# A hybrid attention block on one core: transfers issued in program order, value products in three parts, one product moved from VectorE to GpSimd

## The chip, the cores and the metric

The kernel runs on one core of a Trainium2 chip. The metric is the device time of one execution in microseconds. Three executions of the kernel before took 2690.57, 2697.05 and 2703.49 us; their median is 2697.05 us.

## What is computed

One layer of a transformer-like block over 2048 tokens of width 1024, all in float32. Cut to what matters here:

```python
def stick_breaking_attention(q, k, v):          # 4 heads, causal, head width 64
    # A[t,s] = sigmoid(z_ts) * prod_{s<j<t} (1 - sigmoid(z_tj)),  z = q.k / sqrt(d)
    ...
def chunked_relpos_attention(q, k, v, rel_bias): # 8 heads, chunks of 64, a band of 576 keys
    probs = jax.nn.softmax(scores, axis=-1)
    out = jnp.einsum('bhcqk,bhckd->bhcqd', probs, vb)
    ...
proj = rmsnorm(x, attn_norm_w) @ w_in
y = group_rmsnorm(concat([y_sb, y_ch, y_cv]), out_norm_w)   # y_cv: a gated depthwise convolution
x = x + y @ w_out
x = x + swiglu(rmsnorm(x, ffn_norm_w), w_gate, w_up, w_down)
```

Products keep nearly float32 accuracy by splitting each operand into a high and a low float16 part and adding three of the four partial products.

## The kernel before

**Two halves.** The host hands the tokens over in reversed order, and the kernel works through them in two halves of 1024 (`HALVES`, L50), each of two groups of 512. Everything up to the first half's output projection runs in one interleaved stage, `weave` (L941): two streams of work are traced piece by piece, and TensorE executes exactly that order, since `tc.manual_schedule(engines={PE})` (L1015) fixes it. VectorE, ScalarE, GpSimd and the SyncE queue that issues all transfers are not fixed: a scheduler in the framework puts their instructions in the order that its own model of time suggests, and may take a load long ahead of the place where the program names it. After `weave` come the first half's feed-forward part, the second half's output projection and its feed-forward part (L1102 to L1106), where nothing is fixed by hand.

**The first stream, `fill` (L900),** holds the projections: for each half V, Q and K of the heads, the convolution, then the first half's output projection. Weights are loaded, scaled and split into two float16 parts by `Weights.split` (L227); the parts go to DRAM (L277) to be read again for the second half (L236). Activations are loaded four tiles at a time by `Rows.ahead` (L435; `x_rows`, `y_rows`, `ffn_rows` say from where), normalised where a gain belongs to them (`rms_rows`, L364) and transposed on TensorE (`to_T`, L321). Q and K parts are stored by `put_parts` (L526), V parts by `v_block` (L535). A small clock counts this stream's TensorE work; `later(after, what)` (L895) traces a step so many of its microseconds further on.

**The second stream, `attend` (L788),** holds the attention: per half 12 heads (4 stick-breaking, then 8 chunked), per head two groups, per group four tiles of 128 queries. It loads K, V and, for chunked heads, a bias at the head's start (L798 to L806), and two arrangements of the queries in four transfers at each group's start (L818). A tile of a stick-breaking head is cut into pieces of up to four key blocks; a chunked tile is one piece. In `weave`, `stage` gives each piece three beats; in each beat every open piece that is due goes one step on, and a third of the piece's share of `fill` is traced. A piece's first products are traced at the start of the third beat of its stage, so two beats after the loads that `attend` named just before it.

**A stick-breaking piece (`stick_tile`, L713):** scores on TensorE, two sigmoids on ScalarE (L730, L731), a running product over the remainders by a scan on VectorE (L733), then the product of sigmoids and shifted remainders, `MUL` (L735, `nc.vector` by L53). The remainder tile `re` starts with a memset on GpSimd (L727). Five beats later the product is transposed on TensorE (L660) and split into a high part by ScalarE (L664) and a low part by VectorE (L669), in `turned`.

**The product with the values (`weighted`, L673)** comes five beats after that. For each key block the high part multiplies V's two parts side by side (128 columns, L679) and the low part multiplies V's high part (64 columns, L684). `put_y` (L689) copies and scales the sum one beat later on ScalarE (L694), and another beat later GpSimd adds its two halves of 64 columns (L696) and the tile's result is stored (L697). Two `yu` buffers and one PSUM bank `av` serve this. A chunked tile's scale `f` (L776) has four buffers.

**The output projection (`out_proj`, L858)** loads the residual `xs` where it reads the accumulator (L868, two buffers) and stores the sum at once (L872).

Of the kernel before, what the change touches and what calls it, by code (L numbers as in the profile page):

```python
# [9 lines left out]
F32 = mybir.dt.float32  # L10
# [5 lines left out]
ALU = mybir.AluOpType  # L16
# [24 lines left out]
def trunk(ctx: ExitStack, tc: tile.TileContext, x, anw, w_in, qnw, knw, biasx, conv_w, onw, w_out,  # L41
# [10 lines left out]

    MUL = nc.vector  # L53
    SH_T = ("k c", dict(k=KT))
# [61 lines left out]
    def acc():  # L116
        return bank("acc", 2)
# [86 lines left out]
    class Weights:  # L204
# [22 lines left out]
        def split(self, n):  # L227
# [43 lines left out]
            for i, raw in enumerate(tiles):  # L271
                yield 1.5
                w = wp.tile([128, 2, D], F16, name="w16", tag="w16")
                nc.scalar.activation(raw, raw, AF.Copy, scale=sc[:, 0:1] if one else sc[:, i:i + 1])  # L274
                nc.scalar.copy(w[:, 0, :], raw)  # L275
                nc.gpsimd.tensor_tensor(w[:, 1, :], raw, w[:, 0, :], ALU.subtract)  # L276
                nc.sync.dma_start(wd[key][i], w)  # L277
                made.append(w)
# [204 lines left out]
    def y_rows(H, groups):  # L483
# [5 lines left out]
        return Rows(H, groups, fetch)  # L489

    def behind(what):
        if stream.paced:
            later(0.8, what)
        else:
            what()
# [12 lines left out]

    def proj_N(H, groups, units, use, prep=None):

        for g in groups:
            hh, hl = H.get(g, (None, None))
            for t in range(0, 4, 2):
                if prep is not None:
                    yield from prep.need(g, t)
                    hh, hl = H[g]
                o, bk = acc()
                steps = chain.from_iterable(
                    mm3(o[:, s * 256:(s + 1) * 256], lambda k, cs=cs: hh[:, k, cs],
                        lambda k, cs=cs: hl[:, k, cs], lambda k: units[k // 4][0][:, k % 4],  # L520
                        lambda k: units[k // 4][1][:, k % 4], KT, 0.33)
                    for s, cs in ((s, slice((t + s) * 128, (t + s + 1) * 128)) for s in range(2)))
                yield from prep.beside(steps) if prep is not None else steps
                behind(bk.read(lambda g=g, t=t, o=o: use(g, t, o)))

    def put_parts(src, pair, g, d, scale):  # L526
# [5 lines left out]
        for part in range(2):  # L532
            nc.sync.dma_start(d[pair, half, part][:, c:c + GRP], st[:, part, :])

    def v_block(H, groups, W, c0, head0, prep=None):  # L535
# [8 lines left out]
        def use(g, t, o):  # L544
# [7 lines left out]
            b = c // 128 + t  # L552
            nc.sync.dma_start(vd[head0, hf][:, b:b + 2], st)

# [51 lines left out]
    def conv_block(H, groups, W, b, between=None):  # L606
# [28 lines left out]
        def finish(g, t1):  # L635
# [6 lines left out]
            for i in range(4):  # L642
                nc.sync.dma_start(ydr[g * 4 + i][:, 768 + 128 * b:896 + 128 * b], yc[:, i * 128:(i + 1) * 128])

# [28 lines left out]
    def weighted(av, wh, wl, vs, first, last):  # L673


        n = len(vs)

        def high(i):
            nc.tensor.matmul(av, wh[:, i * 128:(i + 1) * 128], vs[i], start=first and i == 0,  # L679
                             stop=last and i == n - 1 > 0)  # L680

        high(0)
        for i, v in enumerate(vs):
            nc.tensor.matmul(av[:, :HD], wl[:, i * 128:(i + 1) * 128], v[:, 0, :], start=False,  # L684
                             stop=last and n == 1)
        for i in range(1, n):
            high(i)

    def put_y(T, head, av, f):  # L689
        av, bk = av  # L690
        yield
        bk.done = True
        u = ap.tile([128, 2 * HD], F32, name="yu", tag="yu")
        nc.scalar.activation(u, av, AF.Copy, scale=f)  # L694
        yield
        nc.gpsimd.tensor_tensor(u[:, :HD], u[:, :HD], u[:, HD:], ALU.add)  # L696
        nc.sync.dma_start(ydr[T][:, head * HD:(head + 1) * HD], u[:, :HD])  # L697

# [11 lines left out]
    def open_av():  # L710
        return bank("av", 1, 2 * HD)

# [41 lines left out]
    def chunk_tile(T, head, K, k0, Q, V, cols, bias):  # L754
# [3 lines left out]
        def steps():  # L758
# [16 lines left out]
            yield 2  # L775
            f = small(1, "f")  # L776
            nc.vector.reciprocal(f, tot)
# [54 lines left out]
    def y_norm(T, yt, gain, tmp):  # L832
# [10 lines left out]
        nc.gpsimd.tensor_tensor(yt, yt, gain, ALU.mult)  # L843
        nc.sync.dma_start(ynd[T], yt)

# [12 lines left out]
    def out_proj(H, groups, W, prep, rows):  # L858

        for g in groups:  # L860
            for cb in range(4):
                cc = slice(cb * 256, (cb + 1) * 256)
                units = W.get(("o", cb))

                def use(g, t, o, cb=cb, cc=cc):
                    xs = xp.tile([128, 2, 256], F32, name="xs", tag="xs", bufs=2)
                    T = g * 4 + t
                    nc.sync.dma_start(xs, x[T * 128:T * 128 + 256, cc].rearrange("(b p) c -> p b c", p=128))  # L868
                    nc.vector.scalar_tensor_tensor(xs, o.rearrange("p (b c) -> p b c", b=2),
                                                   descale(("o", cb), 0), xs, op0=ALU.mult, op1=ALU.add)  # L870
                    for b in range(2):
                        nc.sync.dma_start(x1d[T + b][:, cc], xs[:, b, :])  # L872

                yield from proj_N(H, [g], units, use, prep if cb == 0 else None)
                if g == groups[-1] and cb in (1, 2) and len(groups) > 1:
# [130 lines left out]
    with tc.tile_pool(name="ap", bufs=1) as ap0:  # L1006

        class _Pool:
            BUFS = dict(k=2, q=4, be=5, re=2, w2=8, wth=3, wtl=3, v=2, vst=1, yu=2, bias=2)

# [3 lines left out]
        ap = _Pool()  # L1014
        with tc.manual_schedule(engines={mybir.EngineType.PE}):  # L1015
            weave()
# [123 lines left out]
```

## Time and profile before

| | |
|---|---|
| median of three runs | 2697.05 us |
| the profiled execution's own time | 2698.59 us |
| its span in the trace | 2696.8 us |
| TensorE busy (matmuls) | 2526.3 us, 94% of the span |
| VectorE, ScalarE, GpSimd busy | 1458.7, 1074.8, 398.8 us |
| granted TensorE clock, mean | 0.982 |
| transfers | 1178, 294 MB, all issued by SyncE's queue |

The page divides the span by engine, names the waits of each engine and what ended them, and groups instructions by source line. A busy share is an average over stages with different limits: `weave` takes the first 1206 us, and TensorE is busy there for about 1053 us; in the remaining 1491 us it is idle for only some 18 us.

### The profile page before, as it was taken

The page shows a single profiled execution, that of the slowest core. Times are in us where ns is not written, and L with a number is a line of the kernel's source. Part 1 is how long each engine was busy: PE and PEld are TensorE (multiplying, and loading weights), DVE is VectorE, ACT ScalarE, POOL GpSimd, SP SyncE. Part 2 cuts the span into 40 slices and gives each one's busy share as a digit, 9 for nine tenths or more (in the row PEclk, how much of TensorE's full clock was granted, in tenths as well). Part 3 has the DMA queues.
Part 4 walks back from the last instruction along what each step waited for, and adds up shares of the span by engine and source line. Part 5 has one row for each costly group of instructions (what it writes and reads, how often), then busy time and mean ns, then how long its engine had stood idle before and what let it go on. Part 6 is the DMA issues. An engine that isn't in the chain of part 4 may idle for free.

```text
span 2696.8 us, 41816 instructions
## 1 busy us (share of the span) xinstructions
PE 2526.3 (94%) x16258; PEld 1687.1 (63%) x16258; DVE 1458.7 (54%) x3343; ACT 1074.8 (40%) x1994; POOL 398.8 (15%) x469
## 2 busy tenths in 40 slices
PE   6998889998799888979999999999999999999999
PEld 4477766666686677745555555557865555555556
DVE  6478777689988977834444334334332333223233
ACT  5575756666456776752333333321121111111110
POOL 2234331102312122121111111110000000000000
PEclk9999999999999999989999999999999999999999
DMA  7443444533321356472222233222651111111101
GB/s 260 133 131 100 132 134 143 142 110 124 105 81 43 97 152 198 120 268 105 94 94 94 94 103 113 90 102 107 223 194 39 47 47 51 66 47 48 47 24 63
DMA packets 245350, 294.31 MB, mean 109 GB/s; under 512 B 77472, under 2 KB 194208, under 8 KB 245152
## 3 DMA queue, kind: packets, MB, share of 16 engines
q1 hardware_dynamic: 245152, 291.65, 33.5%
q8 instruction: 127, 2.08, 0.3%
q14 instruction: 71, 0.58, 0.1%
HBM read 199.30 MB, written 92.27 MB: 108 GB/s over the span
## 4 chain that ended last, share of the span: by engine, by line
PE 38%; DMA 4%; issue 4%; DVE 2%; POOL 1%; ACT 1%; SPq 1%; POOLq 0%; DVEq 0%; ACTq 0%
PE acc L381 7%; PE acc L380 7%; PE acc L379 7%; PE sc L1057 5%; PE sc L1058 5%; PE sc L1059 5%; DMA x1d<-xs 1%; POOL w L276 1%; DMA wr<-in_w_down 1%; DMA wr<-in_w_up 1%; DMA xf<-x1d 0%; PE sc L329 0%; DVE gl L1042 0%; DVE x L1061 0%; DVE wl L314 0%
## 5 line engine op out<-in xcount | busy, mean ns | idle before, releaser
L381 PE MATMUL acc<-hh,w 128*128 128x512 f16 x1728 | 656.3, 380 | 0.8 <-POOL w L276 0.8
L379 PE MATMUL acc<-hh,w 128*128 128x512 f16 x1728 | 656.5, 380 | 0.4 <-ACT hh L332 0.4
L380 PE MATMUL acc<-hl,w 128*128 128x512 f16 x1728 | 656.4, 380 | 0.1
L1038 DVE SCALAR_TENSOR_TENSOR sg<-acc,ds,sg 128x512 f32<-128x512 f32 x88 | 66.0, 750 | 622.9 <-PE acc L381 548.8
L379 PE MATMUL acc<-w,hh 128*128 128x256 f16 x1408 | 391.6, 278 | 5.8 <-ACT w L275 4.2
L380 PE MATMUL acc<-w,hh 128*128 128x256 f16 x1408 | 391.5, 278 | 1.8 <-POOL w L276 1.8
L381 PE MATMUL acc<-w,hl 128*128 128x256 f16 x1408 | 391.0, 278 | 1.5 <-DVE hl L333 0.8
L1061 DVE TENSOR_TENSOR x<-sc,x 128x512 f32<-128x512 f32 x352 | 241.2, 690 | 200.9 <-PE sc L1059 194.1
L381 PEld LDWEIGHTS <-w 128*128 128x128 f16 x1728 | 169.1, 98 | 206.4 <-issue 2.0
L379 PEld LDWEIGHTS <-w 128*128 128x128 f16 x1728 | 169.3, 98 | 184.9 <-issue 7.2
L380 PEld LDWEIGHTS <-w 128*128 128x128 f16 x1728 | 169.2, 98 | 180.3 <-issue 1.1
L1057 PE MATMUL sc<-wh,gh 128*128 128x512 f32 x704 | 278.7, 396 | 3.0 <-DVE x L1061 3.0
L1058 PE MATMUL sc<-wl,gh 128*128 128x512 f32 x704 | 274.4, 390 | 0.0
L1059 PE MATMUL sc<-wh,gl 128*128 128x512 f32 x704 | 274.3, 390 | 0.0
L276 POOL TENSOR_TENSOR w<-wr,w 128x1024 f16<-128x1024 f32 x76 | 163.4, 2164 | 550.6 <-ACT w L275 515.0
L669 DVE SCALAR_TENSOR_TENSOR wtl<-tp,wth 128x512 f16<-128x512 f32 (+3 forms) x384 | 198.4, 532 | 41.8 <-ACT wth L664 40.4
L733 DVE TENSOR_TENSOR_SCAN re<-re,zero 128x512 f32<-128x512 f32 (+3 forms) x160 | 192.6, 1203 | 39.7 <-ACT re L730 39.2
L664 ACT ACTIVATE wth<-tp 128x512 f16<-128x512 f32 (+3 forms) x384 | 173.6, 476 | 87.3 <-PE tp L660 86.0
L1041 ACT CAST gh<-sg 128x512 fp32r<-128x512 f32 x88 | 54.3, 617 | 385.3 <-DVE sg L1038 385.3
L274 ACT ACTIVATE wr<-wr,wsc 128x1024 f32<-128x1024 f32 x76 | 84.4, 1146 | 202.0 <-DVE wsc L263 201.8
L380 PEld LDWEIGHTS <-hh 128*128 128x128 f16 x1408 | 140.5, 100 | 31.7 <-issue 5.5
L679 PE MATMUL av<-v,wth 128*128 128x128 f16 x1104 | 144.0, 224 | 16.3 <-ACT yu L694 16.2
(168 smaller groups left out, 3724.3 us busy)
## 6 DMA issues: line engine op xcount, KB each, us to landing
w<-wd SPq DMA_DIRECT2D x92, 512.0 KB, 4.0
wd<-w SPq DMA_DIRECT2D x76, 512.0 KB, 2.9
wr<-in_w_down SPq DMA_DIRECT2D x44, 512.0 KB, 4.4
q<-qd SPq DMA_DIRECT2D x192, 64.0 KB, 2.3
wr<-in_w_gate SPq DMA_DIRECT2D x22, 512.0 KB, 4.5
wr<-in_w_up SPq DMA_DIRECT2D x22, 512.0 KB, 5.3
xt<-in_x SPq DMA_DIRECT2D x16, 512.0 KB, 5.2
wr<-in_w_in SPq DMA_DIRECT2D x16, 512.0 KB, 5.1
```

Of the source, the lines that this page charges most:

```text
L276: nc.gpsimd.tensor_tensor(w[:, 1, :], raw, w[:, 0, :], ALU.subtract)
L379: nc.tensor.matmul(o, sh(k), mh(k), start=(k == 0), stop=False)
L380: nc.tensor.matmul(o, sh(k), ml(k), start=False, stop=False)
L381: nc.tensor.matmul(o, sl(k), mh(k), start=False, stop=(k == n - 1))
L664: nc.scalar.activation(wh[:, b0 * 128:b1 * 128], tp[:, :(b1 - b0) * 128], AF.Copy, scale=WSC)
L669: nc.vector.scalar_tensor_tensor(wl[:, s], tp[:, :(b1 - b0) * 128], WSC, wh[:, s], op0=ALU.mult, op1=ALU.subtract)
L679: nc.tensor.matmul(av, wh[:, i * 128:(i + 1) * 128], vs[i], start=first and i == 0, stop=last and i == n - 1 > 0)
L733: nc.vector.tensor_tensor_scan(re, re, zero.to_broadcast([128, N]), 1.0 if b == T else e[:, 0:1], ALU.mult, ALU.add)
L1057: nc.tensor.matmul(o, gh[:, cs], wh[:, cc], start=st, stop=False)
L1058: nc.tensor.matmul(o, gh[:, cs], wl[:, cc], start=False, stop=False)
L1059: nc.tensor.matmul(o, gl[:, cs], wh[:, cc], start=False, stop=en)
L1061: nc.vector.tensor_tensor(x1, o, x1, ALU.add)
```

## The change

Seven edits go together. SyncE joins the engines whose order is fixed, so inside `weave` transfers are issued in the order in which the program traces them. A helper `store` traces a store some of the clock's microseconds later (weights 5.0, Q, K and V parts 2.0, convolution output and residual 1.5, normalised output 4.0). `MUL` becomes GpSimd. `weighted` takes three products of 64 columns per key block instead of one of 128 and one of 64, so `av` and `yu` are 64 columns wide. `put_y` loses GpSimd's addition; its store is traced two beats behind the copy instead of one. `yu` has four buffers, `f` eight. In `out_proj` the residual is loaded before the products that it is added to, with three buffers.

```diff
--- before.py
+++ after.py
@@ -50,7 +50,7 @@
     HALVES = [list(range(NG - 1, NG // 2 - 1, -1)), list(range(NG // 2 - 1, -1, -1))]
     HT = NTOK // 2
 
-    MUL = nc.vector
+    MUL = nc.gpsimd
     SH_T = ("k c", dict(k=KT))
     SH_N = ("k c", dict(k=4))
     SH_QK = ("k s c", dict(k=4, s=2))
@@ -274,7 +274,7 @@
                 nc.scalar.activation(raw, raw, AF.Copy, scale=sc[:, 0:1] if one else sc[:, i:i + 1])
                 nc.scalar.copy(w[:, 0, :], raw)
                 nc.gpsimd.tensor_tensor(w[:, 1, :], raw, w[:, 0, :], ALU.subtract)
-                nc.sync.dma_start(wd[key][i], w)
+                store(5.0, wd[key][i], w)
                 made.append(w)
 
         def start(self, n, after=0.0):
@@ -488,6 +488,13 @@
 
         return Rows(H, groups, fetch)
 
+    def store(after, dst, src):
+
+        if stream.paced:
+            later(after, lambda: nc.sync.dma_start(dst, src))
+        else:
+            nc.sync.dma_start(dst, src)
+
     def behind(what):
         if stream.paced:
             later(0.8, what)
@@ -506,7 +513,7 @@
                            lambda k: hl[:, k, :], KT)
             behind(bk.read(lambda g=g, o=o: use(g, o)))
 
-    def proj_N(H, groups, units, use, prep=None):
+    def proj_N(H, groups, units, use, prep=None, pre=None):
 
         for g in groups:
             hh, hl = H.get(g, (None, None))
@@ -515,6 +522,8 @@
                     yield from prep.need(g, t)
                     hh, hl = H[g]
                 o, bk = acc()
+                if pre is not None:
+                    pre(g, t)
                 steps = chain.from_iterable(
                     mm3(o[:, s * 256:(s + 1) * 256], lambda k, cs=cs: hh[:, k, cs],
                         lambda k, cs=cs: hl[:, k, cs], lambda k: units[k // 4][0][:, k % 4],
@@ -530,7 +539,7 @@
         nc.scalar.activation(st[:, 0, :], src, AF.Copy, scale=scale)
         nc.vector.scalar_tensor_tensor(st[:, 1, :], src, scale, st[:, 0, :], op0=ALU.mult, op1=ALU.subtract)
         for part in range(2):
-            nc.sync.dma_start(d[pair, half, part][:, c:c + GRP], st[:, part, :])
+            store(2.0, d[pair, half, part][:, c:c + GRP], st[:, part, :])
 
     def v_block(H, groups, W, c0, head0, prep=None):
 
@@ -550,7 +559,7 @@
                                            op0=ALU.mult, op1=ALU.subtract)
             hf, c = where(g)
             b = c // 128 + t
-            nc.sync.dma_start(vd[head0, hf][:, b:b + 2], st)
+            store(2.0, vd[head0, hf][:, b:b + 2], st)
 
         yield from proj_N(H, groups, units, use, prep)
 
@@ -640,7 +649,7 @@
             nc.scalar.copy(yc[:, :512], tp)
             bk.done = True
             for i in range(4):
-                nc.sync.dma_start(ydr[g * 4 + i][:, 768 + 128 * b:896 + 128 * b], yc[:, i * 128:(i + 1) * 128])
+                store(1.5, ydr[g * 4 + i][:, 768 + 128 * b:896 + 128 * b], yc[:, i * 128:(i + 1) * 128])
 
         u = W.get(("cx", b))
         yield from proj_T(H, groups, u[0], use_gc)
@@ -672,29 +681,21 @@
 
     def weighted(av, wh, wl, vs, first, last):
 
-
         n = len(vs)
-
-        def high(i):
-            nc.tensor.matmul(av, wh[:, i * 128:(i + 1) * 128], vs[i], start=first and i == 0,
-                             stop=last and i == n - 1 > 0)
-
-        high(0)
         for i, v in enumerate(vs):
-            nc.tensor.matmul(av[:, :HD], wl[:, i * 128:(i + 1) * 128], v[:, 0, :], start=False,
-                             stop=last and n == 1)
-        for i in range(1, n):
-            high(i)
+            c = slice(i * 128, (i + 1) * 128)
+            nc.tensor.matmul(av, wh[:, c], v[:, 0, :], start=first and i == 0, stop=False)
+            nc.tensor.matmul(av, wl[:, c], v[:, 0, :], start=False, stop=False)
+            nc.tensor.matmul(av, wh[:, c], v[:, 1, :], start=False, stop=last and i == n - 1)
 
     def put_y(T, head, av, f):
         av, bk = av
         yield
         bk.done = True
-        u = ap.tile([128, 2 * HD], F32, name="yu", tag="yu")
+        u = ap.tile([128, HD], F32, name="yu", tag="yu")
         nc.scalar.activation(u, av, AF.Copy, scale=f)
-        yield
-        nc.gpsimd.tensor_tensor(u[:, :HD], u[:, :HD], u[:, HD:], ALU.add)
-        nc.sync.dma_start(ydr[T][:, head * HD:(head + 1) * HD], u[:, :HD])
+        yield 2
+        nc.sync.dma_start(ydr[T][:, head * HD:(head + 1) * HD], u)
 
     def scores(Q, cols, K, k0, n, diagonal=False):
 
@@ -708,7 +709,7 @@
         return z[:, :n], bk
 
     def open_av():
-        return bank("av", 1, 2 * HD)
+        return bank("av", 1, HD)
 
     def stick_tile(T, head, K, k0, Q, V, cols):
 
@@ -773,7 +774,7 @@
             nc.scalar.activation(s[:, :n * 128], s[:, :n * 128], AF.Exp, bias=nm, scale=qks[:, 1:2],
                                  accum_out=tot)
             yield 2
-            f = small(1, "f")
+            f = sp.tile([128, 1], F32, name="f", tag="f", bufs=8)
             nc.vector.reciprocal(f, tot)
             nc.vector.tensor_tensor(f, f, VS[head], ALU.mult)
             yield 3
@@ -841,7 +842,7 @@
         yv = yt.rearrange("p (n d) -> p n d", d=HD)
         nc.vector.tensor_tensor(yv, yv, r[:, :, None].to_broadcast([128, 16, HD]), ALU.mult)
         nc.gpsimd.tensor_tensor(yt, yt, gain, ALU.mult)
-        nc.sync.dma_start(ynd[T], yt)
+        store(4.0, ynd[T], yt)
 
     def y_norms(half):
         assert traced[half] == 0, (half, traced)
@@ -862,16 +863,22 @@
                 cc = slice(cb * 256, (cb + 1) * 256)
                 units = W.get(("o", cb))
 
-                def use(g, t, o, cb=cb, cc=cc):
-                    xs = xp.tile([128, 2, 256], F32, name="xs", tag="xs", bufs=2)
+                XS = {}
+
+                def pre(g, t, cc=cc, XS=XS):
                     T = g * 4 + t
-                    nc.sync.dma_start(xs, x[T * 128:T * 128 + 256, cc].rearrange("(b p) c -> p b c", p=128))
+                    XS[t] = xp.tile([128, 2, 256], F32, name="xs", tag="xs", bufs=3)
+                    nc.sync.dma_start(XS[t], x[T * 128:T * 128 + 256, cc].rearrange("(b p) c -> p b c", p=128))
+
+                def use(g, t, o, cb=cb, cc=cc, XS=XS):
+                    xs = XS[t]
+                    T = g * 4 + t
                     nc.vector.scalar_tensor_tensor(xs, o.rearrange("p (b c) -> p b c", b=2),
                                                    descale(("o", cb), 0), xs, op0=ALU.mult, op1=ALU.add)
                     for b in range(2):
-                        nc.sync.dma_start(x1d[T + b][:, cc], xs[:, b, :])
-
-                yield from proj_N(H, [g], units, use, prep if cb == 0 else None)
+                        store(1.5, x1d[T + b][:, cc], xs[:, b, :])
+
+                yield from proj_N(H, [g], units, use, prep if cb == 0 else None, pre)
                 if g == groups[-1] and cb in (1, 2) and len(groups) > 1:
                     yield from rows.ahead()
 
@@ -1006,13 +1013,13 @@
     with tc.tile_pool(name="ap", bufs=1) as ap0:
 
         class _Pool:
-            BUFS = dict(k=2, q=4, be=5, re=2, w2=8, wth=3, wtl=3, v=2, vst=1, yu=2, bias=2)
+            BUFS = dict(k=2, q=4, be=5, re=2, w2=8, wth=3, wtl=3, v=2, vst=1, yu=4, bias=2)
 
             def tile(self, shape, dt, name, tag):
                 return ap0.tile(shape, dt, name=name, tag=tag, bufs=self.BUFS[tag])
 
         ap = _Pool()
-        with tc.manual_schedule(engines={mybir.EngineType.PE}):
+        with tc.manual_schedule(engines={mybir.EngineType.PE, mybir.EngineType.SP}):
             weave()
 
     fp = ctx.enter_context(tc.tile_pool(name="fp", bufs=1))
```

## Rows read from the trace of the kernel before

**Rows 1.** By stage: busy us (instructions) of PE, PEld, DVE, ACT, POOL; granted clock
```profile
90.00:286.00 196.00, 177.52 (x1490) 133.19 (x1489) 149.73 (x269) 132.53 (x251) 66.28 (x90) 0.97 0.39 120
286.00:532.00 246.00, 223.91 (x1915) 167.91 (x1913) 178.79 (x667) 158.77 (x371) 64.08 (x104) 0.97 0.45 132
532.00:935.00 403.00, 358.61 (x3117) 269.33 (x3116) 366.68 (x667) 244.39 (x456) 88.95 (x110) 0.97 0.30 93
935.00:1152.00 217.00, 191.29 (x2011) 165.13 (x2010) 171.64 (x654) 158.30 (x376) 47.85 (x89) 0.98 0.53 156
```

**Rows 2.** TensorE, waits, whole execution: us in total, times, longest
```profile
PE tp L660 <- DVE wtl L669: 54.4, 37, 4.6
PE sc L329 <- DVE xt L373: 17.2, 2, 15.0
PE av L679 <- ACT yu L694: 16.2, 10, 3.5
...
PE sc L704 <- DMA q<-qd: 0.8, 1, 0.8
```

**Rows 3.** The same, second half's stick-breaking heads, 532 to 935 us
```profile
PE tp L660 <- DVE wtl L669: 22.9, 15, 4.6
PE tp L600 <- DVE wtl L669: 5.9, 4, 2.9
...
PE tp L660 <- DVE be L735: 3.5, 2, 1.9
```

**Rows 4.** The same, first half's stick-breaking heads, 90 to 286 us
```profile
PE tp L660 <- DVE wtl L669: 12.2, 7, 3.9
```

**Rows 5.** The product on VectorE (L735) in those two stretches: busy us (instructions)
```profile
90.00:286.00 196.00, 36.77 (x48) 0.97 0.39 120
532.00:935.00 403.00, 75.62 (x111) 0.97 0.30 93
```

**Rows 6.** By line: busy us, mean ns of one | idle before, releasers
```profile
L735 DVE TENSOR_TENSOR be<-be,re 128x512 f32<-128x512 f32 x112 | 86.0, 768 | 8.4 <-DVE re L733 0.5 <-ACT be L731 0.3
...
L694 ACT ACTIVATE yu<-av,f 128x128 f32<-128x128 f32 x128 | 46.7, 365 | 33.6 <-DMA ydr<-yu 19.2 <-PE av L679 8.2 <-issue 5.0
...
L579 POOL TENSOR_TENSOR qs<-qk 128x512 f32<-128x512 f32 x32 | 36.4, 1138 | 41.0 <-ACT qk L577 40.8
...
L373 DVE SCALAR_TENSOR_TENSOR xt<-xt,rry,gain 128x1024 f32<-128x1024 f32 x16 | 22.6, 1433 | 0.1
...
L777 DVE RECIPROCAL f<-tot 128x1 f32<-128x1 f32 x128 | 20.4, 159 | 37.4 <-ACT yu L694 28.3 <-ACT s L773 7.5
...
L368 ACT ACTIVATE junk<-xt 128x1024 bf16<-128x1024 f32 x16 | 16.9, 1056 | 3.6 <-DMA xt<-in_x 3.4
```

**Rows 7.** TensorE timeline, one product with the values (four blocks): start, us
```profile
642.08 0.22 PE L679 MATMUL av<-v,wth 128*128 128x128 f16 x1
642.14 0.28 PE L684 MATMUL av<-v,wtl 128*128 128x64 f16 x4
642.26 0.33 PE L679 MATMUL av<-v,wth 128*128 128x128 f16 x3
642.42 0.27 PE L379 MATMUL acc<-w,hh 128*128 128x256 f16 x1
```

**Rows 8.** What SyncE's queue waited for at the tiles' results, whole execution
```profile
SPq L697 <- POOL yu L696: 320.4, 133, 15.0
```

**Rows 9.** SyncE queue timeline, two places: start, us for all issues
```profile
35.59 0.88 SPq L478 DMA_DIRECT2D xt<-in_x  x2
...
664.60 2.39 SPq L818 DMA_DIRECT2D q<-qd  x4
```

**Rows 10.** Transfers: count, KB each, median us from issue to landing
```profile
q<-qd SPq DMA_DIRECT2D x192, 64.0 KB, 2.3
...
xt<-in_x SPq DMA_DIRECT2D x16, 512.0 KB, 5.2
```

**Rows 11.** Durations of the product on VectorE: minimum, median, longest, ns
```profile
L735 DVE TENSOR_TENSOR be<-be,re x160: 274/691/2372, 98.2 to 936.3; 128x512 f32<-128x512 f32 x112, 128x128 f32<-128x128 f32 x16, 128x256 f32<-128x256 f32 x16, 128x384 f32<-128x384 f32 x16
```

## The prediction

> **What bounds the kernel now.** I read the stages first [rows 1], then TensorE's waits [rows 2 to 4], then who holds whom up. Behind the interleaved stage TensorE is idle for only 18 of 1491 us, and no edit but the earlier residual load reaches there; so the change is decided in the first 1206 us. In the four attention stretches TensorE is idle for 196 - 177.5 = 18.5, 246 - 223.9 = 22.1, 403 - 358.6 = 44.4 and 217 - 191.3 = 25.7 us, in all 110.7, and its granted clock is 0.97 to 0.98 [rows 1]: some stretches run at 1.2 instead of 2.4 GHz, which by 0.03 x (196 + 246 + 403) + 0.02 x 217 costs up to 30 us more. That is the room for a gain. Most of the waits end with VectorE: 54.4 us for a transpose bank that the low part's subtraction (L669) frees [rows 2]. In the second half's stick-breaking stretch VectorE is busy for 366.7 of 403 us, 91%, in the first half's for 76% [rows 1]. Next come 16.2 us in which the value product waits for ScalarE's copy of the tile before. For query loads TensorE waits 0.8 us in all [rows 2]: the order of the transfers costs it next to nothing now, so program order alone has almost nothing to win there.
>
> **The change part by part.** The sum is made against the profiled execution's 2698.6 us, 1.5 above the median shown.
>
> *The product to GpSimd.* 160 instructions leave VectorE, 36.8 and 75.6 us in the two stick-breaking stretches [rows 5]. VectorE falls there from 76 to 58% and from 91 to 72%. On GpSimd a product of this shape takes 1.14 us instead of 0.77 [rows 6]; 112 full ones add some 130 us to an engine that is busy for 89 of 403 us [rows 1], and the result is wanted five beats (several us) later, so those beats hide the longer latency. If other GpSimd work stood before the product for longer than that, its transposes would be late instead. Waits on VectorE in the two stretches: 22.9 + 5.9 + 3.5 [rows 3] + 12.2 [rows 4] = 44.5 us. The bounds are 0 and all of it. I take two thirds, -30, since the chunked stretch at 179 of 246 us, 73% VectorE, still leaves TensorE idle for 22 us. Half of the clock's 18 us there comes back: -9.
>
> *Copy, store and buffers.* ScalarE's copy (L694) itself stood 19.2 us behind stores of the two buffers, and VectorE's reciprocal 28.3 us behind that copy [rows 6], with everything queued after it. Four buffers for `yu`, eight for `f` and no addition on GpSimd remove both. I take all of the 16.2 us of [rows 2], and half of the L669 waits outside the stick-breaking stretches, 54.4 - 22.9 - 12.2 = 19.3: together -26 (bounds 0 and -36), and a third of the chunked stretches' 12 us of clock, -4.
>
> *Three narrow products.* Eight products for four blocks take 642.42 - 642.08 = 0.34 us; the four narrow ones begin 0.12 us apart from first to following line, 30 ns each [rows 7]. After: 3 x 30 = 90 ns a block instead of 0.34 / 4 = 85. For 1104 blocks about +5. The columns per block stay 192, so a gain is left out; above, at the mean 42 ns of all eight, +45.
>
> *Transfers in program order, heads and groups.* Now the queries are issued when their buffers come free. After, the four transfers of a group stand two beats ahead of the first product. They take the queue 2.39 us [rows 9] and land 2.3 us after issue [rows 10]: the last is there 1.8 + 2.3 = 4.1 us after the queue comes to the first. At a head's start in the second half four K, two V and a bias transfer stand before them, some seven at 0.6, so 8.2 us; in the first half 6.3. Against that: the queue waits at each tile's result [rows 8]. The store is now traced three beats after the last product, while the copy (0.37 us) ends about 1 us after it (an estimate). A beat is a third of a piece: 217 us / 64 tiles / 3 = 1.1 us. So the queue passes the store 2.3 us before TensorE comes to that place, and head starts lie a good beat later: a lead of 3.6 us, plus the two beats 5.9. Inside a head nothing is short; second-half heads are short by 2.3 (8 chunked) and about 2 (4 stick-breaking), first-half ones by up to 0.5: 18 + 8 + 4 = +30. With no lead at all it is 100, with a lead over long store-free stretches 0 (as now).
>
> *The activations' loads.* Of the 16 input tiles those of the second half go out from 35.59 us on [rows 9], hundreds of us before use. After, they go out where `Rows.ahead` stands. Until the first transposes the path is then two issues (0.9), landing (5.2) [rows 10], two squares (2 x 1.06), the small steps of the root (2.5, an estimate) and the scaling (1.43) [rows 6]: 12 us, against some 6 us of lead and interleaving at two places (6 short each), less where it runs in one go (the second half's first group and the feed-forward rows: 6 to 7 each), and 2 to 3 at the normalised rows and the end: 12 + 13 + 5 = +30, between 15 and 50.
>
> *Stores and weights.* Deferred stores cost the queue the same time; weights are loaded two blocks ahead (some ten us), so their order is covered by that distance. The earlier residual load saves at most a few us: nothing. Where TensorE pauses for loads, VectorE and ScalarE catch up, so part of the waits on them that I left standing goes: -20 of the 15 + 10 + other small ones.
>
> Sum: -39 - 30 + 5 + 30 + 30 - 20 = -24. 2698.6 - 24 = 2674.6, call it 2674.
>
> The Trainium skill (DMA: Bandwidth & Descriptors, Rules for kernel authors) tells to issue a transfer early and wait for it late; the kernel before does that [rows 9], and this change goes the other way. By that rule alone the loads' +60 would stand and the reordering bring nothing.
>
> **The rivals.** *Late loads decide, slower.* If the lead at head starts is 0.6 instead of 3.6 us, because the stores of Q and K parts or a late copy hold the queue, each of the 24 heads pays some 2 us more: 80 instead of 30, and the activations 50 instead of 30: -24 + 50 + 20 = +46, 2744. It decides once more than about half of the lead is gone. For it: 320 us of waiting at L697 today [rows 8]. Against it: GpSimd's addition, which caused that wait, goes.
>
> *GpSimd and VectorE shut each other out, slower.* A product on VectorE has taken 2372 ns where the median is 691 [rows 11]: something held it for longer than its own length. If each product on GpSimd held VectorE for its whole 1.14 us, VectorE's work in the second half's stretch would be 366.7 - 75.6 + 111 x 1.14 = 418 us; at today's 91% that needs 459, so +56 instead of the -28 I counted there: 2698.6 - 24 + 84 = 2758. Against it: the median shows that most products were not held up. The Trainium skill (SBUF — State Buffer, Who interferes with whom) states such an exclusive port for a GpSimd instruction that reads the memory and a VectorE one with two inputs there; by that rule the scan and the product would exclude each other, and the one long row agrees with it, the median does not.
>
> *Even.* Half of the gain and the loads as counted, or the reverse: 2698.
>
> *Loads hidden.* The queue runs far ahead where no store stands: 5 for heads, 15 for activations: -24 - 25 - 15 = -64, 2634.
>
> **How the numbers follow.** A run can tell this kernel from no change from about 0.5% on, 13 us. Forecast (2674, its own range 2635 to 2684) 0.33; loads hidden 0.14; even 0.18; late loads 0.25; shut out 0.10. So faster 0.47, same 0.18, slower 0.35. The likeliest case is the forecast. The range from 2615 to 2750 takes in the hidden loads with the products at no cost and the late loads; most of the shut-out case and the far ends lie outside.
>
> **What would show it.** Right: waits of a transpose on L669 in the stick-breaking stretches down to about a third; the 16.2 us on L694 gone; VectorE's busy time there near 113 and 291 us; the value products' blocks at 0.36 us; new waits of a score product on query or K transfers of about 30 us, at head starts, and of the first transposes on the scaling (L373) of about 30 more. Wrong: such transfer waits near 80 us or near none; longer scans (L733) on VectorE; transposes waiting for GpSimd's product.

## The result, and the profile after

The changed kernel takes 2787.06 us (median of four runs, 2783.24 to 2792.33), the kernel before beside it 2700.27: a ratio of 1.0329, with a 95% interval from 1.0295 to 1.0363. It is 87 us slower; the forecast was 2674 us, the range ended at 2750. The profiled execution's span went from 2696.8 to 2790.5 us, 93.7 more.

Of these, the page counts 31.8 us as longer TensorE work (2526.3 to 2558.1 us busy, for the same columns, at a mean granted clock of 0.972 instead of 0.982) and 61.9 us as idle time. By stretch, each from the first score product of its first head to that of the next stretch, the last one to the last score product:

| us | start | 1st half, stick | 1st half, chunked | 2nd half, stick | 2nd half, chunked |
|---|---|---|---|---|---|
| before | 90.7 | 195.3 | 246.2 | 403.5 | 203.3 |
| after | 94.7 | 188.9 | 263.9 | 422.0 | 252.5 |

The same stretches of after by stage: length, then busy us (instructions) of PE, PEld, DVE, ACT and POOL, the granted clock, the transfers' share and GB/s. They answer to [rows 1]:

```profile
94.00:284.00 190.00, 173.50 (x1621) 131.79 (x1620) 123.06 (x217) 128.73 (x249) 102.70 (x110) 0.99 0.40 125
284.00:548.00 264.00, 227.38 (x2151) 169.53 (x2150) 182.32 (x663) 153.13 (x365) 43.45 (x45) 0.97 0.41 123
548.00:970.00 422.00, 362.69 (x3529) 272.71 (x3527) 332.51 (x555) 248.93 (x468) 203.85 (x187) 0.95 0.31 96
970.00:1218.00 248.00, 190.31 (x2106) 159.99 (x2107) 163.00 (x621) 138.53 (x338) 25.64 (x28) 0.88 0.46 140
```

Only the first stretch is shorter. The worst is the last, which has short heads. Cut alike, from its first to its last score product (before, then after), TensorE idles there for 58 instead of 26 us, and its own work takes 17 us longer at a granted clock of 0.88 instead of 0.97:

```profile
935.70:1139.10 203.40, 177.90 (x1856) 152.74 (x1854) 163.11 (x633) 150.64 (x358) 46.25 (x84) 0.97 0.55 162
969.50:1222.20 252.70, 194.89 (x2165) 163.74 (x2166) 166.61 (x634) 142.13 (x347) 26.14 (x29) 0.88 0.46 138
```

A stretch that waits also gets more time at 1.2 instead of 2.4 GHz, so it pays twice.

Of the 31.8 us of longer TensorE work, 11.9 have nothing to do with the transfers. They lie behind the last score product, where the granted clock is 0.99 in both kernels: the 2112 float32 products of the down-projection (the feed-forward part's product with `w_down`), which no edit touches, take some 5 ns longer each, 11 us in all. One of their three lines, before and after (count | busy us, mean ns):

```profile
L1058 PE MATMUL sc<-wl,gh 128*128 128x512 f32 x704 | 274.4, 390 | 0.0
```

```profile
L1065 PE MATMUL sc<-wl,gh 128*128 128x512 f32 x704 | 277.9, 395 | 0.0
```

Over all three lines the mean is 397 ns in each of the nine runs of this document that have the narrow products, the copy without addition and the larger buffers, and 392 in each of the five that do not. Which of these edits does it, and how, no run shows.

TensorE's waits in after, whole execution (us in total, times, longest), to be held against [rows 2]:

```profile
PE sc L705 <- DMA q<-qd: 46.0, 17, 6.7
PE sc L329 <- DVE xt L373: 32.8, 4, 14.4
PE sc L329 <- DVE xf L373: 23.5, 3, 10.2
PE sc L705 <- DMA ydr<-yu: 18.7, 5, 6.5
PE tp L669 <- DVE wtl L678: 13.8, 18, 2.3
PE tp L669 <- POOL be L736: 10.2, 8, 3.8
...
PE av L687 <- ACT yu L696: 5.3, 6, 1.9
```

The old waits did shrink: the transposes wait 13.8 instead of 54.4 us for the low part on VectorE, though 10.2 us for GpSimd's product are new, and the value products 5.3 instead of 16.2 for the copy. In their place stands the first score product of a group (L705), which waits 46.0 + 18.7 us for queries; the profile puts the 18.7 down to a store's transfer, but in the head shown below, one of these, the queries' own issues end only 2.1 us before the product starts, so they are counted here too. The two rows at L329 are the first transposes of scaled activations. Counted in TensorE's timeline, its gaps at the first score product of a group come to 49.0 us at the starts of the 16 chunked heads (40.0 of them in the second half, 5.0 a head), 11.4 at those heads' second groups and 6.4 in the second half's stick-breaking heads: 66.8 us, against 2.3 before.

One head's start shows how it comes about. First SyncE's queue (start, us for all issues), then TensorE at the same head (start, duration, line; in brackets the idle time before):

```profile
1080.77 4.11 SPq L698 DMA_DIRECT2D ydr<-yu  x2
1084.97 0.86 SPq L494 DMA_DIRECT2D x1d<-xs  x2
1085.88 0.46 SPq L799 DMA_DIRECT2D k<-kd  x1
...
1090.46 0.50 SPq L807 DMA_DIRECT2D bias<-in_rel_bias  x1
1091.00 2.37 SPq L819 DMA_DIRECT2D q<-qd  x4
```

```profile
1088.63 0.27 PE L381 MATMUL acc<-w,hl 128*128 128x256 f16 x1
1095.44 0.43 PE L705 MATMUL sc<-k,q 128*128 128x320 f16 x1 [6.54 <-DMA ydr<-yu]
```

The queue stands at two results' stores until 1080.77 + 4.11 = 1084.88, issues the stores of two residual sums and comes to the head's first load at 1085.88. Its eleven issues (four K, two V, a bias, four query transfers) end at 1091.00 + 2.37 = 1093.37, 7.5 us later. The first product starts at 1095.44, 9.56 us after the first issue. TensorE was there 6.54 us earlier, at 1088.90: the loads had 3.0 us and needed 9.6. Over the eight chunked heads of the second half they had 4.1 us on average (2.0 to 6.0) and needed 9.1. What the queue waited for at the tiles' results (it was 320.4 us [rows 8]), and the queries' time from issue to landing (it was 2.3 us [rows 10]):

```profile
SPq L698 <- ACT yu L696: 404.3, 130, 13.1
```

```profile
q<-qd SPq DMA_DIRECT2D x192, 64.0 KB, 2.8
```

### The profile page after: what moved, and what is told of

It is laid out like the page before. It is cut to its first block, busy times and chain, and to the rows that moved or that the text cites. A ratio compares the mean times of both kernels' runs of the same rounds, so it can differ in the third digit from the quotient of the medians.

```text
span 2790.5 us, 43938 instructions
## 1 busy us (share of the span) xinstructions
PE 2558.1 (92%) x17362; PEld 1703.0 (61%) x17362; DVE 1406.0 (50%) x3183; ACT 1065.0 (38%) x1994; POOL 502.0 (18%) x437
## 5 line engine op out<-in xcount | busy, mean ns | idle before, releaser
L734 DVE TENSOR_TENSOR_SCAN re<-re,zero 128x512 f32<-128x512 f32 (+3 forms) x160 | 215.3, 1345 | 76.9 <-ACT re L731 76.6
L736 POOL TENSOR_TENSOR be<-be,re 128x512 f32<-128x512 f32 (+3 forms) x160 | 182.2, 1140 | 276.9 <-DVE re L734 123.4
L705 PE MATMUL sc<-k,q 128*128 128x320 f16 (+4 forms) x384 | 126.5, 334 | 68.8 <-DMA q<-qd 46.0
```

The lines of the kernel that those rows point to most:

```text
L734: nc.vector.tensor_tensor_scan(re, re, zero.to_broadcast([128, N]), 1.0 if b == T else e[:, 0:1], ALU.mult, ALU.add)
L736: MUL.tensor_tensor(be[:, 0:N], be[:, 0:N], e[:, 0:N], ALU.mult)
```

## The experiments

My theory after the result was that the fixed order of the transfers costs all of the loss, most of it at the heads' and groups' loads, and that the other edits gain little. The rivals: the GpSimd product itself costs time, by holding up VectorE's scans (B); the narrow products and the copy do (C); or the deferred stores do.

**e1: the change with SyncE's order left free.**

```diff
-        with tc.manual_schedule(engines={mybir.EngineType.PE, mybir.EngineType.SP}):
+        with tc.manual_schedule(engines={mybir.EngineType.PE}):
```

> The changed kernel with one part undone: SyncE leaves the fixed order again (the stores' delays, GpSimd's product, the narrow products and the buffers stay). Theory A (the fixed order of the transfers costs the 87 us and more, the rest gains a little): about 2680, between 2650 and 2700, and waits of score products on query loads under 3 us. Rival B (GpSimd's product holds VectorE and its own queue, the order only moves waits about): about 2770. Rival C (the narrow products and the copy cost): about 2770 as well.

Measured: 2694.05 us, ratio to before 0.9999 [0.9989, 1.0008], clock 0.987. Its waits on TensorE, with no row for queries:

```profile
PE tp L669 <- DVE wtl L678: 35.4, 30, 4.9
PE sc L329 <- DVE xt L373: 17.0, 3, 14.4
PE sc L329 <- DVE xf L373: 13.0, 2, 9.4
```

This one word is worth 93 us. All the other edits together, in a free order, leave the time as it was. In the traces the last score product ends at 1123.1 us in e1 and at 1139.1 in before, so they do gain 16 us there; 9 of these are lost again behind it, where the down-projection's products are slow as in after.

**e3: the fixed order alone.** The kernel before with SyncE in the fixed order, the delayed stores and the early residual load, but with its products, copy, buffers and VectorE product. In terms of after:

```diff
-    MUL = nc.gpsimd
+    MUL = nc.vector
...
-        yield 2
-        nc.sync.dma_start(ydr[T][:, head * HD:(head + 1) * HD], u)
+        yield
+        nc.gpsimd.tensor_tensor(u[:, :HD], u[:, :HD], u[:, HD:], ALU.add)
+        nc.sync.dma_start(ydr[T][:, head * HD:(head + 1) * HD], u[:, :HD])
```

> The kernel before with the transfers' part alone: SyncE in the fixed order, the delayed stores and the early residual loads; product on VectorE, two products per block, GpSimd's addition and two yu buffers as before. Theory A: 2790 to 2830, because GpSimd's addition holds the results' stores and with them the queue even longer than in the changed kernel. Rivals B and C: about 2700 to 2720.

Measured: 2804.99 us, 1.0393 [1.0371, 1.0416]. Here TensorE's waits for queries are:

```profile
PE sc L713 <- DMA q<-qd: 49.4, 19, 5.3
...
PE sc L713 <- DMA ydr<-yu: 27.6, 6, 7.5
```

So the order alone costs more than the whole change; the other edits give 18 us of it back.

**e2: the change with the product on VectorE** (`MUL = nc.vector` in after).

> The changed kernel with one part undone: the product of sigmoids and remainders back on VectorE. Theory A: 2785 to 2810, since VectorE gets 113 us of work back and the late transfers stay. Rival B: 2730 or less, with the second half's stick-breaking stretch back from 422 to about 404 us. Rival C: about 2787.

Measured: 2784.82 us, 1.0325 [1.0309, 1.0342], the same as after. In the fixed order the engine of the product makes no difference, and the 18 us of e3 come from the rest: the narrow products, the copy without an addition, and the buffers. The time is also what rival C let expect, but e1 and e3 rule C out.

**e4: heads' and groups' loads a group ahead, order fixed.** The loads in `attend` become functions, and the next group's queries, or the next head's K, V, bias and queries, are traced after the third of a group's four tiles (`t` runs from 3 down to 0):

```diff
+    def ahead_of(half, groups, head, n):
+        if n == 0:
+            QQ[half, head, groups[1]] = load_q(half, head, groups[1])
+            return
...
+            K, V, bias = KVB.pop((half, head), None) or load_head(half, groups, head)
...
+                if t == 1:
+                    ahead_of(half, groups, head, n)
```

> The changed kernel with the fixed order kept, but K, V, bias and queries of the next group or head are issued after the third of the four tiles of the group before. Theory A, in its narrow form (what costs is that these loads stand too close to their use): waits of score products on transfers fall from 69 us to under 15, the time to 2700 to 2730, what is left being the activations' loads. If the fixed order costs in another way (the queue held by stores, activations' loads): 2760 or more.

Measured: 2743.3 us, 1.0170 [1.0153, 1.0187]. From 1.0329 that is 1.6%, 43 us. Waits:

```profile
PE sc L329 <- DVE xt L373: 37.9, 4, 15.4
PE sc L329 <- DVE xf L373: 23.8, 3, 12.0
PE sc L705 <- DMA q<-qd: 16.6, 6, 5.4
```

The waits for queries fall from 46.0 to 16.6 us, those on the activations stay. Neither range is met: more was left than I had expected for these loads alone, and e7 and e10 show what.

**e7 and e10: the activations early too, and the heads' loads earlier still.** e7 adds to e4 that activation tiles are traced ahead: those of the next group when the second pair of the present ones is taken up, the first ones of the next half, of the output projection and of the feed-forward part, with the gain, a block of products or more before they are wanted; e10 moves the heads' loads of e7 from behind the third tile to behind the first.

```diff
+            rows[half + 1].early()
...
-                if t == 1:
+                if t == 3:
```

> The changed kernel with the fixed order kept, the heads' and groups' loads a group ahead, and also the activations' loads ahead: the next 512 tokens' four tiles when the second pair of the present ones is taken up, the next stage's first four tiles and its gain row one or two projections early. If the rest of the fixed order's price is these loads: waits of the first transposes on the scaling (L373) fall from 62 to about 30 us (14 at the start and what the kernel before also had) and the time from 2743 to about 2710. If it is the queue standing at stores: 2735 to 2745.

> The fixed order with all loads ahead, the heads' and groups' loads now issued after the first of the four tiles of the group before instead of the third. If the 24 us that are left over the order-free kernel are still lateness in the second half's chunked heads (19 us of waits on query loads there): those waits under 5 us and 2695 to 2705. If it is something else in the order: 2715 to 2720.

Measured: e7 2718.62 us, 1.0096 [1.0080, 1.0112]; e10 2689.61 us, 0.9997 [0.9987, 1.0007]. e7's waits, then e10's:

```profile
PE sc L329 <- DVE xt L373: 25.1, 4, 15.2
PE sc L719 <- DMA q<-qd: 21.2, 9, 4.7
PE sc L329 <- DVE xf L373: 11.6, 2, 8.2
```

```profile
PE sc L329 <- DVE xt L373: 22.1, 2, 15.0
PE sc L329 <- DVE xf L373: 12.3, 2, 8.8
PE sc L719 <- DMA q<-qd: 5.0, 2, 2.7
```

By the ratios, e7 gives back 0.7% (20 us) and e10 1.0% (27 us). A third tile's end was not early enough for the short heads; a first tile's is. e7 lies between the two times that I had named, e10 5 us below the better of its own. With everything loaded that early, the fixed order costs nothing any more, and this with the stores still in their places: the stores' delay is not a cost by itself as long as the loads stand far enough ahead.

**e5: only the product on GpSimd, in before.**

```diff
-    MUL = nc.vector
+    MUL = nc.gpsimd
```

> The kernel before with one part alone: the product of sigmoids and remainders on GpSimd, transfers in the scheduler's order, all else as before. If the prediction's term for VectorE's relief holds: about 2656 (39 less). If the waits on the low part's subtraction do not come from VectorE's load (they only pass to GpSimd's product and its queue, as the order-free run with 2694 for all other parts together suggests): 2690 to 2710, with the second half's stick-breaking stretch at 403 us or longer, and new waits of transposes on GpSimd's product.

Measured: 2687.85 us, 0.9988 [0.9978, 0.9998]: 3 us where I had counted 39. Two views show where a part of the relief went: VectorE's waits for GpSimd's squares (us in total, times, longest) and its scan (count | busy us, mean ns | idle before), in before and then in e5:

```profile
DVE qa L583 <- POOL qs L579: 19.3, 16, 3.3
...
L733 DVE TENSOR_TENSOR_SCAN re<-re,zero 128x512 f32<-128x512 f32 (+3 forms) x160 | 192.6, 1203 | 39.7 <-ACT re L730 39.2
```

```profile
DVE qa L583 <- POOL qs L579: 52.1, 26, 3.6
...
L733 DVE TENSOR_TENSOR_SCAN re<-re,zero 128x512 f32<-128x512 f32 (+3 forms) x160 | 216.2, 1352 | 64.8 <-ACT re L730 62.4 <-POOL yu L696 1.3 <-POOL re L727 0.9
```

The scans of the same shapes grow from 1203 to 1352 ns, 23.6 us over all 160. The growth sits in few of them: of the 112 full ones in e5, the 30 that by the trace's times ran beside a product on GpSimd took 1704 ns on average (2344 at most), the 56 beside which GpSimd did nothing 1249. And VectorE stands 32.8 us longer at the sums of squares (L583): GpSimd squares the Q and K parts too (L579), and a square now starts 2.25 us after the copy that it reads, in before 1.19.

**e6: only the narrow products, the copy without an addition, `yu` 4 and `f` 8, in before.**

```diff
-        u = ap.tile([128, 2 * HD], F32, name="yu", tag="yu")
+        u = ap.tile([128, HD], F32, name="yu", tag="yu")
...
-            f = small(1, "f")
+            f = sp.tile([128, 1], F32, name="f", tag="f", bufs=8)
```

> The kernel before with one part alone: three narrow products per block, the copy and store without GpSimd's addition, four yu buffers and eight for f; transfers in the scheduler's order, product on VectorE. If the prediction's terms hold (the 16 us of waits on the copy go, half of 19 us of others, 5 us for the narrow products): about 2675. If a wait removed there only turns up at the next releaser: 2690 to 2700.

Measured: 2690.2 us, 0.9985 [0.9975, 0.9995], 4 us. The value products still wait for the copy, 11.7 us where [rows 2] has 16.2:

```profile
PE av L678 <- ACT yu L687: 11.7, 7, 4.5
```

The chunked stretches became shorter, 246.2 to 239.9 and 203.3 to 191.1 us, the stick-breaking ones longer, 195.3 to 197.1 and 403.5 to 405.8, in all 14 us less. Behind the last score product 6 us are lost again (1557.7 to 1563.5), with TensorE busy for 12.5 us more: the down-projection's products are slow here too, 395 ns on the line shown above.

**e8 and e11: the squares on ScalarE.** If the queue on GpSimd is what ate e5's gain, taking the squares from it must set the gain free. e11 does it in before, e8 in e5.

```diff
-            nc.gpsimd.tensor_tensor(sq[:, :512], s, s, ALU.mult)
+            nc.scalar.activation(sq[:, :512], s, AF.Square)
```

> The kernel before with the product on GpSimd, and the squares of the chunked heads' Q and K (L579) moved from GpSimd to ScalarE. With the product alone VectorE's sum of squares (L583) waited 52 us for GpSimd instead of 19. If that wait in VectorE's queue is where the relief went: those waits under 10 us, the second half's stick-breaking stretch under 400 us, 2660 to 2678. If the transposes' waits have another cause (the order of VectorE's queue, the pieces' own chain): 2683 to 2692, like the product alone.

> The control for the run with the squares on ScalarE: the kernel before with the squares there, product on VectorE. If the two moves need each other (the product's relief was lost in waits for GpSimd's squares): the squares alone give under half of the 34 us, 2675 to 2692. If the squares alone did it all: 2655 to 2662.

Measured: e8 2656.08 us, 0.9878 [0.9863, 0.9893]; e11 2674.68 us, 0.9920 [0.9906, 0.9933]. VectorE's waits for the squares in e8, then in e11:

```profile
DVE qa L583 <- ACT qs L579: 3.8, 6, 1.3
```

```profile
DVE qa L583 <- ACT qs L579: 2.1, 4, 0.9
```

The waits are gone in both. Two thirds of e8's gain are the squares' own, so e11 meets neither of its expectations; the product on GpSimd adds 0.42% (11 us) once they are out of its way, against 0.12% when they are in it. Some 28 of the 39 us counted for it are missing even so; the slower scans are a candidate, but no run parts them from the rest. ScalarE also takes 0.64 us for a square where GpSimd took 1.14 [rows 6]; these runs do not part the emptier queue from the faster engine.

**e9 and e12: the parts put together.** e9 is e8 with e6's edits, in the free order; e12 is e10 with the squares on ScalarE, so the whole change with its loads mended.

> The run before this one with the narrow products, the copy without addition and the larger buffers as well, transfers in the scheduler's order. If the small gains add up: 5 us under that run, so 2660 to 2682, faster than both kernels. If the order-free run's 2694 shows that they do not add up: about 2690.

> The changed kernel with all loads ahead as in the last run, and the squares on ScalarE. If the fixed order costs nothing once the loads stand early: 2655 to 2670, as in the scheduler's order. If the squares' gain hangs on the scheduler's order: 2680 to 2690.

Measured: e9 2668.5 us, 0.9924 [0.9909, 0.9938]; e12 2657.98 us, 0.9855 [0.9840, 0.9871]. e12 beats both kernels and is not to be told from e8, whose interval it overlaps. From e9 it differs in the transfers alone, and it is 0.7% faster: with the loads early, the fixed order is no worse than the scheduler's. e9 lies in the range given for gains that add up, yet it is worse than e8 by 0.46%, so in the free order e6's edits cost some 12 us beside e8's, though they gained 4 in before. The traces show where. From the first to the last score product e8 takes 1011.1 us and e9 1012.1; the 12 us lie behind it, at the same granted clock (e8, then e9):

```profile
1101.50:2653.70 1552.20, 1523.03 (x7475) 919.26 (x7472) 556.52 (x980) 341.49 (x487) 114.52 (x58) 0.99 0.27 94
```

```profile
1102.10:2666.20 1564.10, 1535.68 (x7501) 921.46 (x7498) 558.11 (x980) 341.11 (x488) 112.17 (x52) 0.99 0.27 93
```

TensorE is busy there for 12.7 us more, and 11 to 12 of these are the down-projection's slower products (389 against 395 ns on the line shown above).

## Why the prediction was wrong

**The step that failed** is the term for the heads' and groups' loads, +30 us: its lead. It had the right mechanism and the right place, but it let the queue pass the last store 2.3 us ahead of TensorE and come to the loads 5.9 us before the first product. Over the chunked heads of the second half it was 4.1 us, at the head shown 3.0, and the loads took 9.1 and 9.6 us where 8.2 were counted: the eleven issues take 7.5 us together at that head, and queries land 2.8 us after issue instead of 2.3. So a chunked head of the second half is 5.0 us short on average, not 2.3, and these heads wait 40.0 us, not 18. The first half's heads pay 9.0 us instead of 4, and second groups, taken as covered, 11.4; the stick-breaking heads, with 6.4 us for 8, were right. The term also put no price on the clock, which fell where TensorE waited. e4 and e10 give back 43 + 27 = 70 us, where I had 30. The late-loads rival named this cause (0.6 us and two beats, 2.9 in all) and, with 80 us, nearly this price; its total of 2744 was too low because it kept the gains. Against it I had set that GpSimd's addition goes; the queue's waits at the results rose all the same, from 320.4 to 404.3 us, now for the copy.

**The activations' loads**, +30 us between 15 and 50, were right: e7 gives 20 us by its ratio, and the waits at L329 are 32.8 + 23.5 in after against 17.0 + 13.0 in e1, 26.3 more. With the 70 us that is 90, and e1 measured 93 for the order as a whole.

**The product on GpSimd** was counted at -39 and gave 3 us alone, 11 with the squares out of its way. The transposes' waits on VectorE fell only from 54.4 to 37.1 us in e5, and 8.7 us of waits for GpSimd's product came in:

```profile
PE tp L660 <- DVE wtl L669: 37.1, 28, 5.1
...
PE tp L660 <- POOL be L735: 8.7, 8, 3.4
```

VectorE's busy time in the second half's stick-breaking stretch came to 332.5 us in after, where I had 291: the products' 75.6 us left, the slower scans took 18.6 back (133.8 to 152.4 us), and the other 22 are spread over the rest of VectorE's work. I weighed that mechanism as a rival with a whole product's length (1.14 us) for each, and gave it a tenth; it acts, but with 0.15 us on the average scan, since only some of them meet a product. The Trainium skill (SBUF — State Buffer, Who interferes with whom) states that a VectorE instruction with two inputs in that memory contends with a GpSimd instruction that reads it; the growth of the scans from 1203 to 1352 ns agrees with this in sign. That the squares wait behind the products in GpSimd's queue, and VectorE behind the squares, I had not counted at all: I looked at who waits for the product, not at what queues behind it. e5's waits show it, and the product gains more with the squares gone (e8 against e11).

**The copy and the buffers**, -30, gave 4 us alone (e6) and 18 in the fixed order (e3 against e2). In after the value products' waits are down to 5.3 us, as said, but in e6 only to 11.7: most of the 16.2 us did not hang on the two buffers. Both gains are what is left after the 11 us by which the down-projection became slower with these edits.

**Behind the interleaved stage** I put the change at nothing but the residual load, since TensorE is idle there for 18 us only. That looked at idle time alone: TensorE's own work there grew by 11.9 us, as shown with the result.

**The narrow products** themselves were right. Four blocks take 842.14 - 841.79 = 0.35 us, before 0.34 [rows 7]; one product with the values in after:

```profile
841.79 0.19 PE L687 MATMUL av<-v,wth 128*128 128x64 f16 x1
...
842.14 0.27 PE L379 MATMUL acc<-w,hh 128*128 128x256 f16 x1
```

**The overlap**, -20, is partly there: the transposes' waits on VectorE fall from 35.4 us in e1 to 13.8 in after while TensorE pauses for loads. What I left out is the other sign of such pauses, the clock: 17 of the 31.8 us by which TensorE's work grew lie in the last stretch, at a granted clock of 0.88. e10, with hardly such a pause left, is at 1.00 in that stretch and at 0.986 in all, after at 0.972.

The prediction quoted the Trainium skill (DMA: Bandwidth & Descriptors, Rules for kernel authors) for issuing a transfer early and waiting for it late, and said that by this rule alone the loads' +60 would stand and the reordering bring nothing. Here e4, e7 and e10 bear it out: 1.0329, 1.0170, 1.0096, 0.9997 as the loads move forward.

## What to carry to other kernels

When a queue's order is fixed to the program's, a load must be traced as far ahead as the queue can be held up by the stores before it, plus every issue that stands between, plus the landing; count that for the shortest stretch of work, not for the usual one. Before moving work to an idle engine, look at what already queues there and who waits for that: moving the squares away was worth twice as much as moving the products in. Gains measured alone do not add up here (e6 and e8 against e9), so a version is chosen by running it; and an edit's cost may lie in a stage that it does not touch, so compare the traces stage by stage to the end.

## What was not expected of the hardware

- A scan of the same shapes on VectorE takes 1203 ns on average with the products on VectorE and 1352 ns with those products on GpSimd (e5); in after 1345:

```profile
L734 DVE TENSOR_TENSOR_SCAN re<-re,zero 128x512 f32<-128x512 f32 (+3 forms) x160 | 215.3, 1345 | 76.9 <-ACT re L731 76.6
...
L736 POOL TENSOR_TENSOR be<-be,re 128x512 f32<-128x512 f32 (+3 forms) x160 | 182.2, 1140 | 276.9 <-DVE re L734 123.4
```

- One queue's issues add up: the eleven loads of a head, all small, take SyncE 7.5 us, more than the 2.8 us that a query transfer needs from issue to landing.
- Short pauses cost clock as well: in the stretch with 5 us of waiting a head the granted clock is 0.88 in after, and TensorE spends 194.9 us on its products from the first to the last score product. e10, with the same products and hardly a wait for queries, spends 173.3 us on them at 1.00. In between lie e7, idle for 34 us of this stretch at a clock of 0.97, and e4, idle for 43 us at 0.92. The row of e10:

```profile
933.40:1123.50 190.10, 173.32 (x2167) 150.56 (x2165) 164.38 (x637) 147.53 (x355) 29.18 (x28) 1.00 0.59 172
```

- The same float32 products of the down-projection, at a granted clock of 0.99 each time, take 392 ns on average in five runs and 397 in the nine with the narrow products and their buffers, 11 us in all; the cause is open.
